# Three column blocks of an out-projection kept in PSUM until the third mixer joins, and x moved on GpSimd's queue

## The chip, the cores and the metric
The kernel runs on one core of one Trainium2 chip. The metric is the time of one execution in microseconds (us), and less is better. The time before is the median of three runs.

## The reference
An encoder of two layers works on 512 tokens of width 1024. Each layer has two halves: a mixer half, with three token mixers side by side, and a feed-forward half, dense in layer 0 and two of eight experts in layer 1. The change concerns the end of the mixer half, from the merged mixers to the residual x.

```python
def rms_norm(x, g):
    xf = x.astype(jnp.float32)
    y = xf * lax.rsqrt(jnp.mean(xf * xf, axis=-1, keepdims=True) + EPS)
    return (y * g.astype(jnp.float32)).astype(x.dtype)
...
    merged = jnp.concatenate([
        rms_norm(o_ssm, out_norm[:e1]),
        rms_norm(o_mla.astype(h.dtype), out_norm[e1:e2]),
        rms_norm(o_fox.astype(h.dtype), out_norm[e2:]),
    ], axis=-1)
    return merged @ w_out
...
    for i in range(DEPTH):
        ada = c_act @ w_ada[i] + b_ada[i]
        sh1, sc1, g1, sh2, sc2, g2 = jnp.split(ada, 6, axis=-1)

        h = modulate(rms_norm(x, norm_mix[i]), sh1, sc1)
        mix = hybrid_mixer(h, cos, sin, w_in[i],
...
        x = x + g1[:, None, :] * mix

        h = modulate(rms_norm(x, norm_ffn[i]), sh2, sc2)
        j = i // 2
        if i % 2 == 0:
            ff = swiglu(h, ffn_w_gate[j], ffn_w_up[j], ffn_w_down[j])
        else:
            ff = moe_ffn(h, moe_w_router[j], moe_b_router[j], moe_w_gate[j], moe_w_up[j], moe_w_down[j])
        x = x + g2[:, None, :] * ff
```

The mixers are S5 (o_ssm, width 256), latent attention (o_mla, 384) and forgetting attention (o_fox, 384). Together they make 1024 columns, which are eight blocks of 128: blocks 0 and 1 are S5, 2 to 4 latent attention, 5 to 7 forgetting attention.

## The kernel before
x is kept with its features on the partitions: eight column blocks of 128 partitions by 512 tokens, 256 KB each. A product in full precision is three matmuls (mm3, L397 and L400 to L402): the weights' high half wh by the activations' high half mg0 and low half mg1, and the weights' low half wl by mg0. The weights come raw from DRAM on SyncE's queue into wr, ScalarE casts them to wh (L383), and VectorE subtracts to get wl (L384); there are two buffers each of wh and wl.

The out-projection is done in two parts, because two mixers are ready before the third.
- In the first part, step "w,d" of a list written by hand (SEQ), for each column block d: a load of x's block from where the layer's input lies (xsrc, L1273), 15 matmuls over the five blocks of the mixers that are ready, a gated add of x (L1280) and a write of the sum into a DRAM tensor xs (L1281). The loads and writes are issued on ScalarE's queue. Three tiles, sA, sB and sC, take turns.
- The third mixer (latent attention) is normalised and merged by g,M (L406 to L417, L953, L961 to L963). The sum over its squares is L953, its first reader is L406 on ScalarE.
- In the second part x's eight blocks are loaded from xs (L1300, ScalarE's queue), and for each d nine matmuls over the third mixer's three blocks go into a bank, which is added, gated, into x (L1309).

Behind it, layer 0 squares x (L493), adds the squares (L495) and sums them over the partitions on TensorE (L498) for the next norm. In layer 1 the router is fed block by block (route: L1594 the router's product, L1596 transposes, L1598 to L1603 what reads them). moe_ahead, called ahead of the second part, loads the router's weights on GpSimd's queue (L1553), makes vec from the adaLN values (L1557, L1559), ws from the weights (L1561), multiplies ws by ones (L1565, ws's bank is read into brt by L1567), and transposes vec into vt, which goes through DRAM (L1573 to L1578).

During the last attention units and the out-projection, layer 0 also streams the adaLN weights: 512 KB a load on SyncE's queue, one VectorE instruction each (L478).

PSUM has eight banks, in four tags with 2, 3, 2 and 1 bank: A, B, C and D. A step names its tag, or bank() takes the next one of a cycle. The Tile scheduler orders the instructions of each engine under what the lists and priorities give it; it is the program text that is changed here, and the order follows.

Of the kernel before, what the change touches and what calls it, by code (L numbers as in the profile page):

```python
# [21 lines left out]
P = 128  # L22
D = 1024
L = 512
DEPTH = 2
KD = D // P
# [27 lines left out]
def _most_blocks():  # L54
# [4 lines left out]
    while todo:  # L59
# [12 lines left out]
NIT = NE  # L72
WST = 200
# [31 lines left out]
SEQ = ("""k,BBAD v,BD f,0,B p,0,4,1 f,1,A p,4,4,0 R l s,0 A s,1 m,0 A a,16,25 s,2 f,2,C A s,3 a,25,26 A o m,1 A m,2 a,26,34 g,F,A g,5,D a,34,40 A w,0,C g,M,A w,1,C w,2,C w,3,C w,4,C w,5,A w,6,C w,7,D""",  # L105
       """k,AACC R f,0,B s,0 s,1 v,A l f,1,C s,2 m,0 A A f,2,B s,3 A m,1 A o m,2 A g,F,C g,5,C A g,M,B w,0,A w,1,C w,2,B w,3,C w,4,C w,5,C w,6,C w,7,C""")
# [180 lines left out]
class Net:  # L287
# [889 lines left out]

    def layer_mix(self, l, xsrc, x, xst):

        nc, tc, a = self.nc, self.tc, self.a  # L1180
        v = nc.vector
        with ExitStack() as st:
# [4 lines left out]
            ps = self.norm_sum(x, (0, 2, 4, 6)) if l == 0 else None  # L1187
# [7 lines left out]
            with ExitStack() as st2:  # L1195
# [3 lines left out]
                units, env = [], {}  # L1199
# [71 lines left out]
                def out(d, side):  # L1271
                    xt = env["far"].tile([P, L], FT, tag="s" + "ABC"[d % 3], name="xs", bufs=1)
                    nc.scalar.dma_start(out=xt, in_=xsrc[:, d])  # L1273
                    hi, lo = self.wload(a["wofs"][l, d], 5 * P)
                    ps = self.bank(side)
                    for kk in range(5):
                        k = (5, 6, 7, 0, 1)[kk]
                        s = slice(kk * P, (kk + 1) * P)
                        self.mm3(ps, (hi[:, s], lo[:, s]), tuple(m_[:, k] for m_ in env["mg"]), kk == 0, kk == 4)
                    v.scalar_tensor_tensor(out=xt, in0=ps, scalar=g1[:, d:d + 1], in1=xt, op0=OP.mult, op1=OP.add)  # L1280
                    nc.scalar.dma_start(out=xs[:, d, :], in_=xt)  # L1281

                do = dict(k=gates, v=values, f=fox, p=mats, R=open_far, a=ada, s=s5, o=s5_out, l=mla_low,
                          m=mla, A=att, g=merge, w=out)
# [14 lines left out]
            for k in range(KD):  # L1299
                nc.scalar.dma_start(out=x[:, k], in_=xs[:, k, :])  # L1300
            for d2 in range(KD // 2):
                hi, lo = self.wload(a["wom"][l, d2], 6 * P)
                for d in (2 * d2, 2 * d2 + 1):
                    ps = self.bank()
                    for kk in range(3):
                        c = (d % 2) * 3 + kk
                        s = slice(c * P, (c + 1) * P)
                        self.mm3(ps, (hi[:, s], lo[:, s]), tuple(m_[:, 2 + kk] for m_ in mg), kk == 0, kk == 2)
# [634 lines left out]
```

## Time and profile before

| | |
|---|---|
| time, median of 3 runs | 1590.76 us (1585.99 to 1594.48) |
| profiled execution | 1596.47 us, span 1594.8 us |
| granted TensorE clock, mean | 0.951 |
| TensorE busy | 1473.1 us, 92% |
| VectorE busy | 1108.4 us, 70% |
| ScalarE busy | 794.6 us, 50% |
| GpSimd busy | 154.3 us, 10% |

The profiled execution has its own time. The span is the time from its first to its last instruction, and all the starts below are counted from the span's start. An engine's waiting time stands ahead of the instruction that ended it, with what it is put down to. The clock is in shares of full speed: 1.00 is 2.4 GHz, 0.50 is 1.2 GHz, and a number between is a mean over the window.

### The profile page before, as it was taken

What the parts mean: (1) busy time and instruction counts of PE and PEld (TensorE: products, weight loads), DVE (VectorE), ACT (ScalarE), POOL (GpSimd) and SP (SyncE); (2) the same over time, 40 slices, a digit from 0 to 9 for tenths busy, and PEclk for the clock granted to TensorE, in tenths of its full rate; (3) what the DMA queues carried; (4) which work ended last, traced back from release to release, by engine and by line L of the source; (5) the groups of instructions that cost most, each with busy time, mean ns of one, the idle gap of its engine ahead of it and who ended that gap; (6) DMA issues with size and microseconds to landing.
All of it is one profiled execution on the core that took longest, in us unless ns stands there. A gap on an engine that the chain in (4) does not pass through costs nothing.

```text
span 1594.8 us, 24065 instructions
## 1 busy us (share of the span) xinstructions
PE 1473.1 (92%) x8331; PEld 1223.5 (77%) x8331; DVE 1108.4 (70%) x2522; ACT 794.6 (50%) x1525; POOL 154.3 (10%) x238
## 2 busy tenths in 40 slices
PE   6889888879999999999999999679999999999996
PEld 5877665658888788887878657568878998998894
DVE  7685678766855577555446565678777878878885
ACT  4245368343332233233435862357556766776672
POOL 0312210011000000003111000110000001002002
PEclk7989999989999999999989999789999999999997
DMA  9423432655566656553421006277777878879885
GB/s 351 145 91 132 151 104 75 224 211 158 173 210 193 223 181 224 181 166 106 130 80 55 21 1 204 86 255 283 250 267 282 307 242 299 321 265 334 281 293 195
DMA packets 94720, 308.87 MB, mean 194 GB/s; under 512 B 12144, under 2 KB 12592, under 8 KB 94592
## 3 DMA queue, kind: packets, MB, share of 16 engines
q1 hardware_dynamic: 74880, 253.42, 47.0%
q0 software_dynamic: 12800, 41.26, 7.6%
q10 hardware_dynamic: 6912, 12.59, 2.3%
q8 instruction: 68, 1.11, 0.3%
q14 instruction: 60, 0.49, 0.1%
HBM read 283.43 MB, written 23.79 MB: 193 GB/s over the span
## 4 chain that ended last, share of the span: by engine, by line
PE 55%; DMA 13%; DVE 13%; issue 11%; ACT 6%; POOL 1%; ACTq 0%; SPq 0%; DVEq 0%; POOLq 0%
PE psB L401 5%; PE psB L402 4%; PE psB L400 4%; DMA adw<-in_wada_dram 4%; PE psC L401 3%; PE psC L400 3%; PE psC L402 3%; PE psA L401 3%; PE psA L400 3%; PE psA L402 3%; DMA wr<-in_mw_dram 2%; DVE wl L384 2%; PE psB L1461 2%; DVE adw L478 2%; PE psA L877 1%
## 5 line engine op out<-in xcount | busy, mean ns | idle before, releaser
L383 ACT CAST wh<-wr 128x1024 fp32r<-128x1024 f32 (+4 forms) x402 | 395.4, 993 | 433.8 <-PE psB L401 82.5
L384 DVE TENSOR_TENSOR wl<-wr,wh 128x1024 fp32r<-128x1024 f32 (+4 forms) x402 | 457.7, 1148 | 153.9 <-ACT wh L383 151.0
L478 DVE SCALAR_TENSOR_TENSOR adw<-adw,cact 128x1024 f32<-128x1024 f32 x80 | 97.8, 1223 | 78.2 <-DMA adw<-in_wada_dram 78.0
L877 PE MATMUL psA<-U 65*128 65x128 f32 (+5 forms) x192 | 74.8, 476 | 16.6 <-ACT pr L881 8.5
L1461 PE MATMUL psB<-hgB,wh 128*128 128x432 f32 (+3 forms) x256 | 80.4, 323 | 0.2
L880 DVE TENSOR_REDUCE ms<-psA 128x1 f32<-128x128 f32 (+2 forms) x96 | 46.2, 486 | 49.4 <-PE psA L878 49.0
L1463 PE MATMUL psB<-hgB,wl 128*128 128x256 f32 x256 | 71.2, 284 | 0.6 <-DVE wl L384 0.6
L400 PE MATMUL psB<-fh,wh 128*128 128x512 f32 (+1 forms) x156 | 61.2, 392 | 4.7 <-ACT fh L518 4.7
L881 ACT ACTIVATE pr<-psA,ms 128x128 f32<-128x128 f32 (+2 forms) x96 | 51.9, 544 | 25.2 <-DVE ms L880 25.0
L1461 PE MATMUL psC<-hgB,wh 128*128 128x432 f32 (+3 forms) x192 | 61.2, 324 | 1.7 <-ACT wh L383 1.6
L401 PE MATMUL psB<-fh,wh 128*128 128x512 f32 (+1 forms) x156 | 61.0, 391 | 0.8 <-POOL fh L521 0.5
L402 PE MATMUL psB<-fh,wl 128*128 128x512 f32 (+1 forms) x156 | 60.5, 388 | 0.0
L1461 PE MATMUL psA<-hgB,wh 128*128 128x432 f32 (+3 forms) x184 | 58.9, 326 | 0.2 <-ACT wh L383 0.2
L1463 PE MATMUL psC<-hgB,wl 128*128 128x256 f32 x192 | 54.0, 284 | 3.1 <-DVE wl L384 2.9
L877 PEld LDWEIGHTS psA<-U 65*128 65x128 f32 (+1 forms) x192 | 32.6, 205 | 26.2 <-ACT pr L881 13.0
L1463 PE MATMUL psA<-hgB,wl 128*128 128x256 f32 x184 | 51.8, 283 | 0.3 <-DVE wl L384 0.3
L894 ACT COPY PT<-psB 128x384 f32<-128x384 f32 (+1 forms) x72 | 37.2, 530 | 26.8 <-PE psB L891 26.4
L1461 PEld LDWEIGHTS psB<-hgB,wh 128*128 128x128 f32 x256 | 48.5, 190 | 2.0 <-ACT wh L383 1.1
L1463 PEld LDWEIGHTS psB<-hgB,wl 128*128 128x128 f32 x256 | 48.4, 189 | 1.3 <-DVE wl L384 0.8
L1541 POOL DMA_DIRECT2D yd<-yt x21 | 11.8, 564 | 376.2 <-ACT yt L1531 265.6
L891 PE MATMUL psB<-cst,pr 128*128 128x128 f32 x240 | 42.6, 285 | 5.9 <-ACT pr L881 4.8
L891 PEld LDWEIGHTS psB<-cst,pr 128*128 128x128 f32 x240 | 28.0, 146 | 24.1 <-issue 11.1
(774 smaller groups left out, 4300.5 us busy)
## 6 DMA issues: line engine op xcount, KB each, us to landing
wr<-in_mw_dram SPq DMA_DIRECT2D x158, 512.0 KB, 4.5
adw<-in_wada_dram SPq DMA_DIRECT2D x80, 512.0 KB, 3.5
wr<-in_md_dram SPq DMA_DIRECT2D x80, 512.0 KB, 4.3
wr<-in_fg_dram SPq DMA_DIRECT2D x22, 512.0 KB, 4.0
wr<-in_fu_dram SPq DMA_DIRECT2D x22, 512.0 KB, 4.0
wr<-in_me_dram SPq DMA_DIRECT2D x16, 512.0 KB, 4.6
wr<-in_w_f_dram SPq DMA_DIRECT2D x12, 512.0 KB, 3.5
wr<-in_fd_dram SPq DMA_DIRECT2D x16, 384.0 KB, 3.1
```

Of the source, the lines that this page charges most:

```text
L383: nc.scalar.copy(hi[:, :n], raw[:, :n])
L384: nc.vector.tensor_tensor(out=lo[:, :n], in0=raw[:, :n], in1=hi[:, :n], op=OP.subtract)
L400: mm(ps, a[0], b[0], start=start, stop=False, skip_group_check=shared)
L401: mm(ps, a[0], b[1], start=False, stop=False, skip_group_check=shared)
L402: mm(ps, a[1], b[0], start=False, stop=stop, skip_group_check=shared)
L478: nc.vector.scalar_tensor_tensor(out=w, in0=w, scalar=1.0, in1=self.cact, op0=OP.mult, op1=OP.mult, accum_out=self.ada[l][:, j:j + 1])
L877: nc.tensor.matmul(ps[:, s], U[0:r, 2 + hh, i * P:n], U[0:r, hh, 0:n], start=True, stop=False)
L880: v.reduce_max(out=m, in_=ps[:, s], axis=AX.X, negate=True)
L881: nc.scalar.activation(pr[:, s], ps[:, s], AF.Exp, bias=m, accum_out=ls[:, hh, i:i + 1])
L891: nc.tensor.transpose(ps[:, c * P:(c + 1) * P], pr[:, o:o + P], self.C("ident"))
L1461: mm(ps[:, :2 * C], hi[:, s], h2, start=(kk == 0), stop=False, skip_group_check=True)
L1463: mm(ps[:, C:C + 2 * P], lo[:, s], h2[:, 0:2 * P], start=False, stop=(kk == KD - 1), skip_group_check=True)
```

## The change
In both layers the first part is done in steps for blocks 0 to 4 alone (NWX is 5). For blocks 5, 6 and 7 its 15 matmuls are issued right behind the x loads, by the new out_first, into banks with the tags B, C and A, without the flag that ends a sum. In the second part the nine matmuls of those blocks go on in the same bank, and their gated add takes x from its source. So for three blocks the load of x into a tile of the first part, the gated add there, and the write to xs are gone. All moves of x at this place (loads and writes of the first part, eight loads of the second) are issued on GpSimd's queue.

```diff
@@ -102,8 +104,8 @@
-SEQ = ("""... A w,0,C g,M,A w,1,C w,2,C w,3,C w,4,C w,5,A w,6,C w,7,D""",
-       """... g,M,B w,0,A w,1,C w,2,B w,3,C w,4,C w,5,C w,6,C w,7,C""")
+SEQ = ("""... A w,0,C g,M,A w,1,C w,2,C w,3,C w,4,C""",
+       """... g,M,B w,0,A w,1,C w,2,B w,3,C w,4,C""")
@@ -1175,6 +1177,14 @@
+    def out_first(self, ps, l, d, mg, stop=False):
+
+        hi, lo = self.wload(self.a["wofs"][l, d], 5 * P)
+        for kk in range(5):
+            k = (5, 6, 7, 0, 1)[kk]
+            s = slice(kk * P, (kk + 1) * P)
+            self.mm3(ps, (hi[:, s], lo[:, s]), tuple(m_[:, k] for m_ in mg), kk == 0, stop and kk == 4)
@@ -1270,15 +1280,11 @@
                 def out(d, side):
                     xt = env["far"].tile([P, L], FT, tag="s" + "ABC"[d % 3], name="xs", bufs=1)
-                    nc.scalar.dma_start(out=xt, in_=xsrc[:, d])
-                    hi, lo = self.wload(a["wofs"][l, d], 5 * P)
+                    nc.gpsimd.dma_start(out=xt, in_=xsrc[:, d])
                     ps = self.bank(side)
...
+                    self.out_first(ps, l, d, env["mg"], True)
                     v.scalar_tensor_tensor(out=xt, in0=ps, scalar=g1[:, d:d + 1], in1=xt, op0=OP.mult, op1=OP.add)
-                    nc.scalar.dma_start(out=xs[:, d, :], in_=xt)
+                    nc.gpsimd.dma_start(out=xs[:, d, :], in_=xt)
@@ -1297,15 +1303,21 @@
             for k in range(KD):
-                nc.scalar.dma_start(out=x[:, k], in_=xs[:, k, :])
+                nc.gpsimd.dma_start(out=x[:, k], in_=xs[:, k, :] if k < NWX else xsrc[:, k])
+
+            whole = {}
+            for d in range(NWX, KD):
+                whole[d] = self.bank("BCA"[d - NWX])
+                self.out_first(whole[d], l, d, mg)
             for d2 in range(KD // 2):
                 hi, lo = self.wload(a["wom"][l, d2], 6 * P)
                 for d in (2 * d2, 2 * d2 + 1):
-                    ps = self.bank()
+                    ps = whole[d] if d in whole else self.bank()
...
-                        self.mm3(ps, (hi[:, s], lo[:, s]), tuple(m_[:, 2 + kk] for m_ in mg), kk == 0, kk == 2)
+                        self.mm3(ps, (hi[:, s], lo[:, s]), tuple(m_[:, 2 + kk] for m_ in mg),
+                                 kk == 0 and d not in whole, kk == 2)
```

The lines move down by two above out_first and by some twelve below it: L384 becomes L386, L1281 becomes L1287, L1309 becomes L1321, L1565 becomes L1577.

What the change does to VectorE's order in layer 0, at the third mixer's merge (oM is that mixer's output, ada with adw the adaLN stream, L407 to L417 its norm); before:

```order
L417 SCALAR_TENSOR_TENSOR nr<-ntmp,nr 128x512
L478 SCALAR_TENSOR_TENSOR adw,ada_111<-adw,cact 128x1024
L961 SCALAR_TENSOR_TENSOR oM<-oM,sm_107,nr 128x512 x3
L1280 SCALAR_TENSOR_TENSOR xs<-psA,ada_111,xs 128x512
L384 TENSOR_TENSOR wl<-wr,wh 128x640
L963 TENSOR_TENSOR mg_2836<-oM,mg_2835 128x512 x2
L1280 SCALAR_TENSOR_TENSOR xs<-psC,ada_111,xs 128x512
L963 TENSOR_TENSOR mg_2836<-oM,mg_2835 128x512
L478 SCALAR_TENSOR_TENSOR adw,ada_111<-adw,cact 128x1024
L384 TENSOR_TENSOR wl<-wr,wh 128x768
L1280 SCALAR_TENSOR_TENSOR xs<-psD,ada_111,xs 128x512
L384 TENSOR_TENSOR wl<-wr,wh 128x768
```

and with the change:

```order
L419 SCALAR_TENSOR_TENSOR nr<-ntmp,nr 128x512
L480 SCALAR_TENSOR_TENSOR adw,ada_111<-adw,cact 128x1024
L963 SCALAR_TENSOR_TENSOR oM<-oM,sm_107,nr 128x512 x3
L386 TENSOR_TENSOR wl<-wr,wh 128x640
L965 TENSOR_TENSOR mg_2836<-oM,mg_2835 128x512 x2
L480 SCALAR_TENSOR_TENSOR adw,ada_111<-adw,cact 128x1024
L965 TENSOR_TENSOR mg_2836<-oM,mg_2835 128x512
L386 TENSOR_TENSOR wl<-wr,wh 128x768 x2
L480 SCALAR_TENSOR_TENSOR adw,ada_111<-adw,cact 128x1024
L1321 SCALAR_TENSOR_TENSOR x<-psA,ada_111,x 128x512
```

The three gated adds of blocks 5 to 7 (L1280) are gone; the subtraction for block 7's weights (128x640) stands directly behind L963, which was L961.

TensorE's order in layer 1 around the router's ws (psB_9037 is block 1 of the second part); before:

```order
L400 MATMUL psB_9037<-mg0_8520,wh_9008 128x512
L401 MATMUL psB_9037<-mg1_8521,wh_9008 128x512
L402 MATMUL psB_9037<-mg0_8520,wl_9009 128x512
L1565 MATMUL psC_8973<-ws8_8967,ones_69 128x8 x8
L1571 MATMUL psC_8984<-cst_95,vec_8968 16x128
L1596 MATMUL psA_9048<-cst_95,x_8960 128x128 x4
L1594 MATMUL psD_8996<-wr8_8965,x_8960 128x8 x8
L1596 MATMUL psC_9023<-cst_95,x_8960 128x128 x4
```

and with the change (psA_8957 holds block 7's and psC_8935 block 6's first part):

```order
L402 MATMUL psA_8957<-mg0_8505,wh_8960 128x512
L403 MATMUL psA_8957<-mg1_8506,wh_8960 128x512
L404 MATMUL psA_8957<-mg0_8505,wl_8961 128x512
L1577 MATMUL psC_8880<-ws8_8874,ones_69 128x8 x8
L1583 MATMUL psC_8891<-cst_95,vec_8875 16x128
L402 MATMUL psC_8935<-mg0_8505,wh_8938 128x512
L403 MATMUL psC_8935<-mg1_8506,wh_8938 128x512
L404 MATMUL psC_8935<-mg0_8505,wl_8939 128x512
```

The ws matmuls stood behind all of the first part and two blocks of the second, and now stand behind block 7's first part and ahead of block 6's.

GpSimd's queue in layer 1; before:

```order
L1021 COPY xn<-nld 128x2
L1022 MEMSET xn 128x2
L1553 DMA wr_8965<-in_wr_dram 128x64
L1575 DMA vd<-vt 16x128
L1578 DMA vrow_8990<-vd 128x1024
L1578 DMA vrow_8991<-vd 128x1024
```

and with the change:

```order
L1024 MEMSET xn 128x2
L1283 DMA xs<-xd 128x512 x3
L1287 DMA xs_6441<-xs 128x512 x2
L1283 DMA xs<-xd 128x512 x2
L1287 DMA xs_6441<-xs 128x512 x3
L1565 DMA wr_8872<-in_wr_dram 128x64
L1306 DMA x<-xs_6441 128x512 x5
L1306 DMA x<-xd 128x512 x3
L1587 DMA vd<-vt 16x128
L1590 DMA vrow_8897<-vd 128x1024
L1590 DMA vrow_8898<-vd 128x1024
```

The router's weights (wr) are now issued behind all the writes into xs and ahead of the loads of x; vd and vrow follow these.

## Rows read from the trace of the kernel before

**Rows 1.** The page, part 1: busy time, share of the span and instructions of each engine.
```profile
PE 1473.1 (92%) x8331; PEld 1223.5 (77%) x8331; DVE 1108.4 (70%) x2522; ACT 794.6 (50%) x1525; POOL 154.3 (10%) x238
```

**Rows 2.** Timeline of ScalarE, layer 0: start, us, engine line operation, idle before <-releaser.
```profile
301.18 0.72 ACT L383 CAST wh<-wr 128x640 fp32r<-128x640 f32 x1 [7.02 <-DMA xs<-xs]
...
325.52 5.62 ACTq L1300 DMA_DIRECT2D x<-xs  x8
331.26 0.84 ACT L383 CAST wh<-wr 128x768 fp32r<-128x768 f32 x1 [5.22 <-DMA x<-xs]
```

**Rows 3.** Timeline of TensorE, layer 0, same columns.
```profile
297.31 1.02 PE L953 MATMUL psA<-sq,ones 128*128 128x512 f32 x2
...
314.43 0.80 PE L402 MATMUL psD<-mg,wl 128*128 128x512 f32 x1 [3.12 <-DVE wl L384]
...
319.72 0.63 PE L402 MATMUL psD<-mg,wl 128*128 128x512 f32 x1
320.14 0.45 PE L400 MATMUL psA<-mg,wh 128*128 128x512 f32 x1
...
336.51 0.39 PE L402 MATMUL psB<-mg,wl 128*128 128x512 f32 x1
339.45 1.12 PE L498 MATMUL psA<-sq,ones 128*128 128x512 f32 x2 [2.56 <-DVE sq L495]
342.03 5.49 PE L498 MATMUL psA<-sq,ones 128*128 128x512 f32 x6 [1.45 <-DVE sq L495]
```

**Rows 4.** Windows, layer 0: busy PE, PEld, DVE, ACT, POOL; PEclk, DMA share, GB/s.
```profile
302.00:310.00 8.00, 7.09 (x27) 4.90 (x28) 6.13 (x10) 2.49 (x4) 0.00 (x0) 1.00 0.91 282
315.00:320.00 5.00, 5.00 (x13) 3.91 (x12) 3.85 (x6) 0.00 (x0) 0.00 (x0) 0.50 0.65 212
342.00:347.50 5.50, 5.47 (x6) 1.85 (x6) 0.00 (x0) 0.63 (x1) 0.00 (x0) 0.50 0.21 83
```

**Rows 5.** Timeline of VectorE, layer 0.
```profile
309.76 1.23 DVE L478 SCALAR_TENSOR_TENSOR adw<-adw,cact 128x1024 f32<-128x1024 f32 x1 [1.62 <-DMA adw<-in_wada_dram]
...
312.90 0.74 DVE L1280 SCALAR_TENSOR_TENSOR xs<-psA,ada,xs 128x512 f32<-128x512 f32 x1
...
316.16 0.68 DVE L963 TENSOR_TENSOR mg<-oM,mg 128x512 fp32r<-128x512 f32 x1
...
330.82 0.75 DVE L1309 SCALAR_TENSOR_TENSOR x<-psA,ada,x 128x512 f32<-128x512 f32 x1 [2.23 <-DMA x<-xs]
...
341.29 0.68 DVE L495 TENSOR_TENSOR sq<-sq 128x512 f32<-128x512 f32 x1
```

**Rows 6.** Windows of layer 1, columns as in rows 4.
```profile
740.00:957.00 217.00, 208.33 (x1413) 165.24 (x1412) 121.65 (x356) 121.33 (x303) 31.62 (x62) 0.95 0.20 65
994.00:998.00 4.00, 4.00 (x22) 4.00 (x20) 0.06 (x1) 0.26 (x1) 1.62 (x3) 0.50 0.05 17
```

**Rows 7.** Timeline of TensorE, layer 1.
```profile
990.27 3.58 PE L1565 MATMUL psC<-ws,ones 128*128 128x8 f32 x16 [3.60 <-DVE ws L1561]
...
1020.58 0.31 PE L1596 MATMUL psC<-cst,x 128*128 128x128 f32 x1
```

**Rows 8.** Timeline of VectorE, layer 1.
```profile
974.20 0.73 DVE L1280 SCALAR_TENSOR_TENSOR xs<-psC,ada,xs 128x512 f32<-128x512 f32 x1
...
985.74 0.17 DVE L1557 SCALAR_TENSOR_TENSOR vec<-ada,sm 128x8 f32<-128x8 f32 x1 [1.30 <-DMA xs<-xs]
...
989.99 0.23 DVE L1561 TENSOR_TENSOR ws<-wr,ada 128x64 f32<-128x64 f32 x1 [0.44 <-DMA wr<-in_wr_dram]
```

**Rows 9.** Timeline of GpSimd, layer 1.
```profile
986.35 0.54 POOL L1553 DMA_DIRECT2D wr<-in_wr_dram  x1 [108.78 <-DVE vec L1559]
```

**Rows 10.** Part 6, DMA issues: count, KB each, median us from issue to landing.
```profile
xs<-xs ACTq DMA_DIRECT2D x16, 256.0 KB, 2.7
x<-xs ACTq DMA_DIRECT2D x16, 256.0 KB, 6.4
```

**Rows 11.** Lines of GpSimd: busy time, mean ns of one, idle before and releasers.
```profile
L1389 POOL DMA_DIRECT2D xd<-x x8 | 4.3, 539 | 97.0 <-DVE ada L481 55.1 <-DVE x L1384 41.9
```

More of the change, by code (lines that the diff above doesn't have):

```diff
@@ L72 @@
 NIT = NE
+NWX = 5
 WST = 200
@@ L104 @@
 FIRST = (("w_vu", NVU, FSD), ("w_f0", 256, "B"))
-SEQ = ("""k,BBAD v,BD f,0,B p,0,4,1 f,1,A p,4,4,0 R l s,0 A s,1 m,0 A a,16,25 s,2 f,2,C A s,3 a,25,26 A o m,1 A m,2 a,26,34 g,F,A g,5,D a,34,40 A w,0,C g,M,A w,1,C w,2,C w,3,C w,4,C w,5,A w,6,C w,7,D""",
-       """k,AACC R f,0,B s,0 s,1 v,A l f,1,C s,2 m,0 A A f,2,B s,3 A m,1 A o m,2 A g,F,C g,5,C A g,M,B w,0,A w,1,C w,2,B w,3,C w,4,C w,5,C w,6,C w,7,C""")
+SEQ = ("""k,BBAD v,BD f,0,B p,0,4,1 f,1,A p,4,4,0 R l s,0 A s,1 m,0 A a,16,25 s,2 f,2,C A s,3 a,25,26 A o m,1 A m,2 a,26,34 g,F,A g,5,D a,34,40 A w,0,C g,M,A w,1,C w,2,C w,3,C w,4,C""",
+       """k,AACC R f,0,B s,0 s,1 v,A l f,1,C s,2 m,0 A A f,2,B s,3 A m,1 A o m,2 A g,F,C g,5,C A g,M,B w,0,A w,1,C w,2,B w,3,C w,4,C""")
 ADN = (2, 2)
@@ L1272, in out @@
                     xt = env["far"].tile([P, L], FT, tag="s" + "ABC"[d % 3], name="xs", bufs=1)
-                    nc.scalar.dma_start(out=xt, in_=xsrc[:, d])
-                    hi, lo = self.wload(a["wofs"][l, d], 5 * P)
+                    nc.gpsimd.dma_start(out=xt, in_=xsrc[:, d])
                     ps = self.bank(side)
[L1276 to L1279, printed above, removed]
+                    self.out_first(ps, l, d, env["mg"], True)
                     v.scalar_tensor_tensor(out=xt, in0=ps, scalar=g1[:, d:d + 1], in1=xt, op0=OP.mult, op1=OP.add)
-                    nc.scalar.dma_start(out=xs[:, d, :], in_=xt)
+                    nc.gpsimd.dma_start(out=xs[:, d, :], in_=xt)
                 do = dict(k=gates, v=values, f=fox, p=mats, R=open_far, a=ada, s=s5, o=s5_out, l=mla_low,
```

## The prediction

> **What bounds the kernel now.** The page's first part comes first: TensorE is busy 92% of the span, VectorE 70% and GpSimd 10% [rows 1]. So an edit that leaves the matmuls as they are can pay only where TensorE waits, or where it runs at the lower of its two clock levels (1.2 and 2.4 GHz). Then I read the ends of the two out-projections, where the change sits, engine by engine and in windows; the reader should look for three things.
>
> First, the queue. In layer 0 ScalarE stands at issues of x moves: a cast at 301.18 waits 7.02 us, put down to xs's DMA, and with it the norm's L406 behind it, though TensorE had written the sum that L406 reads by 298.33; later the eight issues at 325.52 hold ScalarE until a cast at 331.26, which is put down to x's DMA [rows 2, 3]. Second, VectorE. TensorE waits 3.12 us for w7's wl (314.43) and then runs at clock 0.50, after 1.00 between 302 and 310 with waits under 1 us [rows 3, 4]. VectorE was held by an adaLN stream instruction that waited 1.62 us for its load, by three merges and by a gated add (312.90) [rows 5]. Behind the out-projection VectorE is 5.07 us late: TensorE ends at 336.90, but the first add into x waits for x until 330.82, so the last sum of squares ends at 341.97, and the norm's matmuls, again at 0.50, end at 347.52 [rows 3 to 5].
>
> Third, layer 1. The router's weights (wr) are loaded when vec is written, vec waits for the writes into xs, and TensorE waits 3.60 us for ws until 990.27; the window behind it stands at 0.50, and so do its neighbours from 990.2 to 1002.7. TensorE ends at 1020.89 [rows 6 to 8].
>
> **The change part by part.** Matmuls and weight loads stay the same in number. Per layer three loads, three writes and three adds of 0.74 us go; that is VectorE's time, and counts only where it stands ahead of a wait. Five loads, five writes and eight x loads go from ScalarE's queue to GpSimd's, which was idle 108.78 us before its next issue in layer 1 [rows 9]. Each plain issue costs GpSimd 0.54 us [rows 11]; 36 cost it 19 us, hidden by that idle time. The whole blocks hold three banks, so blocks 0 to 4 have fewer to turn over in; each needs one for nine matmuls and an add of 0.74 us, and with five banks left (four in layer 1, where the router holds one) I cost that at nothing (uncovered, it would be 0.74 a block, 3.7 us a layer).
>
> *Layer 0, ahead of the third mixer's part.* One gated add, 0.74 us, leaves VectorE in front of w7's wl, and the adaLN load could be earlier by up to its wait of 1.62 [rows 5]. So wl is ready 0.7 to 2.3 us earlier and TensorE waits 0.8 to 2.4 instead of 3.12. Whether the clock falls then is open: at a spacing of 0.42 (319.72 to 320.14) instead of 0.23 (72 matmuls from 320.14 to 336.90) twelve matmuls lose 2.3 us. The third part starts at 320.14 before, and after between 315.5 (all of it) and 319.4 (the least); I take 317.5, about half of each.
>
> *Layer 0, to the norm.* The third part took 16.76 us for its 72 matmuls, eight blocks of 2.1, without a wait that matters: TensorE ends at 332.3 to 336.2, I take 334.3. The x loads no longer wait for writes of blocks 5 to 7. What releases them is the third merge (done at 316.84 before [rows 5], some 0.8 earlier without the add), so they are issued around 316 and land 2.7 us later, like the moves from xs to xs, or 6.4, like the eight at once before [rows 10]: 318.7 to 322.4, about when the first block is ready (319.6). VectorE then follows TensorE and is late by the last add, square and sum alone, some 0.7 us each, 2.1 instead of 5.07. The last sum ends at 334.4 to 338.3, I take 336.4 (341.97 before). The norm's matmuls behind it may keep their 5.49 us or be rid of the half clock. Gain 3.7 to 8.5 us; I take **6**.
>
> *Layer 1.* ScalarE is freed here too, but TensorE has no wait in blocks 3 to 7, so I take nothing. After w4 (986.67, where its wait began, less two blocks of 2.1 and three of 15 matmuls, 3.45 each: 972.2) come the first parts of blocks 5 and 7. Block 7's weights need the buffer of the high half that block 5 frees, and VectorE's wl: I count 1.0 us of waiting, so it ends at 980.1. Meanwhile w4's add, at 974.20 before [rows 8], is the last one written to xs; its write lands 2.7 us after its issue [rows 10], at about 977.2; vec and the wr issue follow, and ws comes 3.6 us on (986.35 to 989.99 before [rows 8, 9]): at 981.2 instead of 990.2. TensorE waits 1.1 us instead of 3.60. The ws matmuls, 3.58 us at half clock [rows 7], take 1.8 at full: 983.0. Block 6 starts in their bank after VectorE has read it: 0.5. From the ws matmuls to its end TensorE took 27.04 us before (993.85 to 1020.89) for six third parts and eight router parts; 4.4 of it went to half clock until 1002.7, so 22.6. After: 983.0 + 0.5 + 3.45 for block 6 + 4.2 for two more third parts + 22.6 = 1013.8, and 0.8 for a cast and x0 that come late: 1014.6, plus h. The kernel before loses 6.2 us by half clock (12.5 us of it); h lies between nothing and that, since waits under 1 us leave 1.00 in layer 0 [rows 4] and waits from 2.56 us on stand ahead of 0.50 [rows 3, 4]. My waits are 0.5 to 1.1 us, nearer to the first; I take h = 1.3. I leave 1 us for router parts that now follow each other more closely and end VectorE's work later. Gain -1 to 5.3; I take **4**.
>
> **Sum:** 6 + 4 = 10 us. The profiled execution of 1596.47 (span 1594.8) becomes 1586.5; it lies 5.7 above the median of 1590.76, from which the same 10 us give **1581**. The bounds, 3.7 - 1 and 8.5 + 5.3, are 2.7 and 13.8 us: 1577 to 1588. Half a per cent, 8 us, is about what can be told from no change here: the runs of before spread over 8.5.
>
> **A rule that speaks against it.** GpSimd's eight issues of L1389 took 0.54 us on average beside a VectorE that is busy 70% of the span [rows 11, 1]. The Trainium skill ("SBUF — State Buffer", sections "SBUF: two separate sides" and "A bandwidth-pool intuition that's wrong") says that the descriptors of a DMA issued from GpSimd are written by GpSimd, which some VectorE operations lock out of a shared port; it gives 620 ns alone and 3100 ns overlapped, and advises ScalarE's or SyncE's queue. By its second figure the eight x loads of layer 0 would be issued over 25 us instead of 4.3 (estimate), and the gain would be gone; the rows agree with the first figure, and none here shows the second.
>
> **The rivals.**
> *One layer only.* The other stall is handed on: in layer 1 the clock falls anyway, h = 6 (for it: wr's 3.6 us stand in the chain whatever frees it, and three waits follow each other; against: the load starts 9 us earlier), or in layer 0 the adaLN loads set w7's wl as now. Gain 3 to 7, 1584 to 1588; I say 1586.
> *No gain to be seen.* Three bank calls fewer per layer deal out all later banks otherwise, and the instructions of layer 1's attention and of the experts move. From 740 to 957 and from 1042 to the end that is 48% of the span. In the first of these TensorE is idle 8.7 us [rows 6]; half as much again, and one half-clock stretch of 4 us as in [rows 6], eats 8 of the 10: 1588 to 1594, I say 1590.
> *Slower: GpSimd's issues are held.* If each waits for two VectorE instructions like the adaLN stream's 1.23 us [rows 5], it takes 0.54 + 2.46 = 3.0 us. Layer 0's eight loads, in order from 316, then land by 316 + 24 + 2.7 = 342.7, and the norm's last sum is done by 344.8, 2.8 later than before. In layer 1 the write of w4 and the wr load stand one behind the other on this queue: ws comes 4.9 us later than I have it, TensorE ends at 1014.6 + 4.9 + 6 = 1025.5, 4.6 later. Together +7: 1598. It decides from 2.7 us an issue, at which layer 0's last x (340.3) gives the last sum of before. Against it: the 0.54 of [rows 11]. Behind these moves on the queue stand only s5w in layer 0 and vd in layer 1, both needed later.
> *More than I think.* Both drops of the clock gone, and the norm's matmuls at full clock: 14 to 18 us, 1573 to 1577.
>
> **How the numbers follow.** Both layers near my values (1577 to 1585) 0.50; one layer only 0.22; no gain to be seen 0.13; slower 0.08; more 0.07. The bound for faster, 1582.8, cuts the first case near its upper quarter: 0.40 of it, all of the last and 0.05 of the second are 0.52. Slower by 8 us, 1598.7, is half of the slow case and a little of the third: 0.06. The rest is 0.42. The range goes from 1573 to 1593 and leaves out the slow case, the worst of the third and a little below the last. The likeliest case's own range is 1577 to 1585.
>
> **What would show it.** Right: in layer 0 no issue on ScalarE's queue ahead of L406, a wait of TensorE for w7's wl under 2.5 us, x landed within 3 us of the first block, the last sum within 3 us of TensorE's end; in layer 1 the wr issue near 977, a wait at the ws matmuls under 2 us and the clock at 1.00 behind it; issues of x moves of 0.5 to 0.6 us. Wrong: issues of 2 us and more; a wait of 3 us at ws or at block 6; clock 0.50 in either stretch; more waits of TensorE in layer 1's attention or in the experts than before.

## The result, and the profile after

The changed kernel took 1574.61 us, the median of four executions (1569.99 to 1585.06); the kernel before, in four beside it, 1592.62. The ratio is 0.9893, with a 95% interval of 0.9858 to 0.9927: 17 us less, and between 12 and 23. Six more executions later (E5 below) gave 0.9892. The profiled execution of the changed kernel took 1585.06 us with a span of 1583.4, the longest of those four.

The page's first part after the change, to stand against [rows 1]:

```profile
PE 1464.8 (93%) x8331; PEld 1217.8 (77%) x8331; DVE 1105.2 (70%) x2516; ACT 795.0 (50%) x1525; POOL 179.3 (11%) x274
```

The same 8331 matmuls kept TensorE busy for 8.3 us less. A matmul takes longer at the lower clock (the norm's last six took 5.49 us at 0.50 [rows 3, 4] and take 2.84 at 1.00, below), so time that the clock costs stands in the busy time, not in the waits.

For a table by stage I cut each execution at the same five instructions of ScalarE: the first square of the third mixer's output in layer 0 (L952, at 286.64 before), the first L406 of the feed-forward norm (347.55), the first L406 of layer 1 (730.25), the first square of the third mixer's output there (955.48) and the last square of the router's parts (1020.92). The windows before (busy time and count of TensorE, its weight loads, VectorE, ScalarE and GpSimd; then granted clock, DMA share, GB/s):

```profile
0.00:286.64 286.64, 239.50 (x1545) 191.33 (x1546) 211.96 (x695) 146.26 (x364) 47.18 (x85) 0.92 0.44 150
286.64:347.55 60.91, 52.63 (x191) 35.58 (x189) 37.30 (x58) 19.20 (x33) 4.21 (x9) 0.89 0.77 262
347.55:730.25 382.70, 376.08 (x1696) 310.31 (x1696) 241.72 (x520) 118.49 (x178) 19.61 (x25) 0.99 0.57 181
730.25:955.48 225.23, 212.73 (x1416) 169.86 (x1418) 130.16 (x375) 126.11 (x312) 32.51 (x62) 0.94 0.20 64
955.48:1020.92 65.44, 61.55 (x305) 51.29 (x301) 35.99 (x59) 20.31 (x34) 2.15 (x4) 0.90 0.43 141
1020.92:1594.80 573.88, 530.59 (x3182) 465.11 (x3182) 451.27 (x818) 364.21 (x607) 48.65 (x53) 0.96 0.78 273
```

And the changed kernel, cut at the same instructions:

```profile
0.00:290.77 290.77, 245.73 (x1545) 195.60 (x1546) 212.86 (x695) 145.93 (x365) 48.71 (x90) 0.89 0.43 148
290.77:344.26 53.49, 48.04 (x191) 34.11 (x189) 35.05 (x55) 19.62 (x33) 11.78 (x22) 0.97 0.79 271
344.26:730.28 386.02, 378.58 (x1696) 312.74 (x1696) 242.22 (x520) 118.41 (x177) 20.41 (x25) 0.98 0.57 180
730.28:945.88 215.60, 203.52 (x1417) 164.10 (x1418) 129.63 (x375) 126.85 (x313) 36.34 (x65) 0.98 0.21 68
945.88:1004.96 59.08, 57.26 (x305) 46.43 (x302) 34.98 (x57) 20.07 (x34) 10.18 (x19) 0.98 0.40 129
1004.96:1583.40 578.44, 531.63 (x3182) 464.84 (x3181) 450.41 (x816) 364.07 (x607) 51.87 (x53) 0.96 0.77 271
```

The two stages that the change was made in are 7.4 and 6.4 us shorter. So is one in which no line was changed: layer 1's norm, mixers and attention, 225.23 to 215.60. Three came out longer: the first by 4.1, layer 0's feed-forward (the third row) by 3.3 and the last by 4.6. The reader should look at the clock beside each length: 0.89 to 0.97, 0.94 to 0.98, 0.90 to 0.98 in the three stages that gained, and 0.92 to 0.89 in the first, in which TensorE's instructions stand in the same order in both.

Now the rows that answer to those of before. ScalarE in layer 0, to stand against [rows 2]:

```profile
301.41 0.72 ACT L385 CAST wh<-wr 128x640 fp32r<-128x640 f32 x1 [3.10 <-PE psC L403]
302.50 0.69 ACT L408 ACTIVATE ntmp<-psA,eps 128x512 f32<-128x512 f32 x1 [0.37 <-PE psA L955]
```

Both wait for TensorE; no x move stands in the queue. TensorE there, against [rows 3]:

```profile
311.53 0.50 PE L404 MATMUL psC<-mg,wl 128*128 128x512 f32 x1 [1.77 <-DVE wl L386]
...
334.40 0.50 PE L404 MATMUL psC<-mg,wl 128*128 128x512 f32 x1 [1.23 <-DVE wl L386]
...
341.38 2.84 PE L500 MATMUL psB<-sq,ones 128*128 128x512 f32 x6 [0.78 <-DVE sq L497]
```

Before, the wait of 3.12 us was for the low half of block 7's weights. Block 7's first part, from 316.21, now has no wait over 0.5 us; the 1.77 us stand in block 6's, and 1.23 came for a low half of the third part, so that together they are 3.00. The norm's last six matmuls took 2.84 instead of 5.49, at the higher clock. VectorE, against [rows 5]:

```profile
324.86 0.75 DVE L1321 SCALAR_TENSOR_TENSOR x<-psA,ada,x 128x512 f32<-128x512 f32 x1 [1.64 <-DMA x<-xs]
...
340.64 0.68 DVE L497 TENSOR_TENSOR sq<-sq 128x512 f32<-128x512 f32 x1
```

TensorE's last block ended at 337.87, and the last sum of squares 3.45 us behind it instead of 5.07. In layer 1 the issue of the router's weights, against [rows 9]:

```profile
968.10 0.54 POOL L1565 DMA_DIRECT2D wr<-in_wr_dram  x1 [2.63 <-DMA xs<-xs]
```

And the ws matmuls, against [rows 7]:

```profile
966.78 0.50 PE L402 MATMUL psA<-mg,wh 128*128 128x512 f32 x1 [0.59 <-ACT wh L385]
...
970.97 1.95 PE L1577 MATMUL psC<-ws,ones 128*128 128x8 f32 x16
```

The wait of 3.60 us is gone, and the sixteen matmuls took 1.95 instead of 3.58 us. The GpSimd lines of x's moves (busy time, mean ns of one, idle before and releasers):

```profile
L1287 POOL DMA_DIRECT2D xs<-xs x10 | 5.4, 544 | 91.0 <-DVE xs L1286 90.8
...
L1306 POOL DMA_DIRECT2D x<-xs x10 | 5.3, 539 | 8.9 <-PE psA L404 8.9
...
L1283 POOL DMA_DIRECT2D xs<-in_xT_dram x5 | 2.7, 539 | 32.1 <-PE psD L857 21.2 <-DVE o L861 7.8 <-DMA xs<-xs 2.9
```

No issue was held: all 36 took 0.54 us on the mean.

### The profile page after: what moved, and what is told of

It reads as the page before. It is cut to its first block, busy times and chain, and to the rows that moved or that the text cites. A ratio compares the mean times of both kernels' runs of the same rounds, so it can differ in the third digit from the quotient of the medians.

```text
span 1583.4 us, 24058 instructions
## 1 busy us (share of the span) xinstructions
PE 1464.8 (93%) x8331; PEld 1217.8 (77%) x8331; DVE 1105.2 (70%) x2516; ACT 795.0 (50%) x1525; POOL 179.3 (11%) x274
## 3 DMA queue, kind: packets, MB, share of 16 engines
q1 hardware_dynamic: 74880, 253.42, 47.1%
## 4 chain that ended last, share of the span: by engine, by line
PE 36%; DMA 5%; DVE 5%; ACT 2%; issue 2%; POOL 0%; DVEq 0%; SPq 0%; ACTq 0%; POOLq 0%
DMA wr<-in_mw_dram 2%; PE psB L1473 2%; PE psB L403 2%; PE psB L404 2%; PE psB L402 2%; PE psC L1473 2%; DVE wl L386 2%; PE psB L1475 2%; PE psA L1473 1%; PE psC L404 1%; PE psC L403 1%; PE psC L402 1%; PE psA L403 1%; PE psA L404 1%; PE psA L402 1%
## 5 line engine op out<-in xcount | busy, mean ns | idle before, releaser
L386 DVE TENSOR_TENSOR wl<-wr,wh 128x1024 fp32r<-128x1024 f32 (+4 forms) x402 | 457.8, 1149 | 155.3 <-ACT wh L385 146.7
L1473 PE MATMUL psB<-hgB,wh 128*128 128x304 f32 (+3 forms) x264 | 83.0, 325 | 0.1
L883 ACT ACTIVATE pr<-psA,ms 128x128 f32<-128x128 f32 (+2 forms) x96 | 51.5, 540 | 16.8 <-DVE ms L882 16.3
L1473 PE MATMUL psC<-hgB,wh 128*128 128x432 f32 (+3 forms) x176 | 56.6, 327 | 2.6 <-ACT wh L385 2.6
L1473 PE MATMUL psA<-hgB,wh 128*128 128x432 f32 (+3 forms) x168 | 53.1, 323 | 2.0 <-ACT wh L385 2.0
L1553 POOL DMA_DIRECT2D yd<-yt x21 | 11.8, 565 | 376.3 <-ACT yt L1543 264.0
L1473 PEld LDWEIGHTS psB<-hgB,wh 128*128 128x128 f32 x264 | 50.3, 191 | 1.9 <-ACT wh L385 1.0
L1475 PEld LDWEIGHTS psB<-hgB,wl 128*128 128x128 f32 x264 | 50.2, 190 | 2.0 <-DVE wl L386 1.5
L1475 PE MATMUL psA<-hgB,wl 128*128 128x256 f32 x168 | 47.4, 285 | 3.1 <-DVE wl L386 3.0
L1475 PE MATMUL psC<-hgB,wl 128*128 128x256 f32 x176 | 49.7, 286 | 0.0
L893 PEld LDWEIGHTS psB<-cst,pr 128*128 128x128 f32 x240 | 29.4, 152 | 21.7 <-issue 12.5
```

The source lines that it names most:

```text
L386: nc.vector.tensor_tensor(out=lo[:, :n], in0=raw[:, :n], in1=hi[:, :n], op=OP.subtract)
L883: nc.scalar.activation(pr[:, s], ps[:, s], AF.Exp, bias=m, accum_out=ls[:, hh, i:i + 1])
L893: nc.tensor.transpose(ps[:, c * P:(c + 1) * P], pr[:, o:o + P], self.C("ident"))
L1473: mm(ps[:, :2 * C], hi[:, s], h2, start=(kk == 0), stop=False, skip_group_check=True)
L1475: mm(ps[:, C:C + 2 * P], lo[:, s], h2[:, 0:2 * P], start=False, stop=(kk == KD - 1), skip_group_check=True)
```

## The experiments

Each was timed beside the kernel before. To read them I took from each profile the three stages named above (layer 0's end, layer 1's attention, layer 1's end) and the experts, as windows between the same instructions. The table gives each one's length and in brackets TensorE's waits in it, which is the window less TensorE's busy time; what is left is busy time of the same matmuls in every row, so where that differs it is the clock. All in us. The kernels with TensorE's old order in layer 1's attention stand above, those with the new one below.

| kernel | layer 0's end | layer 1's attention | layer 1's end | experts |
|---|---|---|---|---|
| before | 60.9 (8.3) | 225.2 (12.5) | 65.4 (3.9) | 573.9 (43.3) |
| E8 banks shifted | 57.9 (9.0) | 219.4 (12.6) | 65.3 (3.9) | 577.0 (46.2) |
| E7 layer 1, banks as before | 62.1 (11.3) | 221.8 (12.7) | 59.4 (3.2) | 574.6 (45.8) |
| E1 layer 1 alone | 64.3 (11.4) | 219.4 (12.7) | 59.2 (3.1) | 578.7 (49.7) |
| E3 queue alone | 57.0 (6.5) | 217.2 (11.9) | 63.9 (4.2) | 572.8 (43.6) |
| E4 hold alone | 54.9 (7.7) | 214.6 (11.9) | 62.4 (3.6) | 574.7 (44.7) |
| E2 layer 0 alone | 52.4 (5.7) | 217.2 (13.0) | 67.0 (7.8) | 577.1 (46.8) |
| changed | 53.5 (5.5) | 215.6 (12.1) | 59.1 (1.8) | 578.4 (46.8) |
| E5 changed, again | 52.5 (5.3) | 215.7 (11.8) | 60.1 (1.9) | 575.8 (45.4) |
| E6 changed, banks as before | 52.7 (5.8) | 218.8 (12.3) | 59.2 (3.1) | 578.0 (46.0) |

**E1: the change in layer 1 alone.** Layer 0 keeps its eight steps and ScalarE's queue:

```diff
-NWX = 5
+NWX = (8, 5)
...
-                    nc.gpsimd.dma_start(out=xt, in_=xsrc[:, d])
+                    (nc.gpsimd if NWX[l] < KD else nc.scalar).dma_start(out=xt, in_=xsrc[:, d])
```

> The change in layer 1 alone; layer 0 as before. The order of TensorE in layer 1's attention is then word for word that of the kernel before. Theory (the two ends of the out-projections gain 7.4 and about 6.5 us, and a new order of instructions in layer 1's attention, which the change in layer 0 brings about, gains another 10): only the second end gains here, 5 to 7 us, ratio 0.996, and the stretch from layer 1's first norm to its merges (730 to 955 us) takes as long as before. Rival (the attention's stretch differs from execution to execution, whatever the order): that stretch comes out up to 10 us shorter in this profile too. Second rival (layer 1's end is given back in the experts): ratio 1.000.

Measured: ratio 1.0015 (0.9989 to 1.0041), median 1593.95 us. Layer 1's end fell to 59.2 us, as the theory has it, and the experts rose to 578.7, as the second rival has it. The attention's stretch, with the old order of TensorE, came out at 219.4 instead of 225.2: so part of the 9.6 us between the first two profiles is chance.

**E2: the change in layer 0 alone**, with NWX of (5, 8).

> The change in layer 0 alone; layer 1's out-projection as before. TensorE's order in layer 1's attention is that of the changed kernel. Theory: 7 us at layer 0's end and about 10 in layer 1's attention, less some 2 in between: 13 to 16 us, ratio 0.991. Rival (the attention's gain is chance): 5 to 7 us, ratio 0.996.

Measured: ratio 0.9969 (0.9944 to 0.9994), median 1584.67. Layer 0's end (52.4) and the attention (217.2) gained what the theory says, but the total is nearer to the rival's. Part of what is missing stands in the experts, 577.1 (3.2 us more than before), as in E1, and part in layer 1's end, 67.0 (1.6 more), where one wait is now twice as long as the 3.60 us of before:

```profile
973.28 3.55 PE L1577 MATMUL psC<-ws,ones 128*128 128x8 f32 x16 [7.32 <-DMA x<-xs]
```

Why it grew was not tried. Much of the rest is the measure: the profile of before that these lengths are held against is of an execution of 1596.47 us, 4.9 above the median of 1591.62 that E2 was timed beside.

**E3: the queue alone.** The eight blocks stay as before:

```diff
-                    nc.scalar.dma_start(out=xt, in_=xsrc[:, d])
+                    nc.gpsimd.dma_start(out=xt, in_=xsrc[:, d])
...
-                    nc.scalar.dma_start(out=xs[:, d, :], in_=xt)
+                    nc.gpsimd.dma_start(out=xs[:, d, :], in_=xt)
...
-                nc.scalar.dma_start(out=x[:, k], in_=xs[:, k, :])
+                nc.gpsimd.dma_start(out=x[:, k], in_=xs[:, k, :])
```

> Only the queue is changed: all moves of x at this place on GpSimd's queue, all eight blocks as before. TensorE's order in layer 1's attention is that of the changed kernel. Theory: the attention's 10 us, and at layer 0's end 1 to 3 us, since ScalarE is no longer held at the issues, but x still waits for the writes of blocks 5 to 7: 10 to 13 us, ratio 0.993. Rival (the blocks held in PSUM do it all): within 3 us of before. Second rival (GpSimd's issues are held while VectorE works): issues of x moves of 2 us and more, slower by 5.

Measured: ratio 0.9954 (0.9933 to 0.9974), median 1584.44. The second rival is out: the 48 issues of x moves took 0.54 us on the mean, and the kernel is not slower. Of the two ends it gains part, 57.0 and 63.9 us, 0.9 and 1.4 us under the shortest of the kernels whose end there is that of before (57.9 and 65.3); the attention is at 217.2.

**E4: the three blocks held, all moves on ScalarE's queue** (the same three lines the other way round in the changed kernel).

> Only the three blocks are held in PSUM; all moves of x stay on ScalarE's queue. TensorE's order in layer 1's attention is that of the changed kernel. Theory: the attention's 10 us, and of the two ends some 4 us each, since x of blocks 5 to 7 needs no write any more, but ScalarE still stands at issues: 16 to 18 us, ratio 0.990, at most 3 us behind the changed kernel. Rival (the queue does it): within 3 us of before.

Measured: ratio 0.9926 (0.9899 to 0.9953), median 1580.25. Both ends lie between before and the changed kernel (54.9, 62.4). By these profiles, one of each, the hold is the larger part, the queue adds to it, and neither does the whole; the intervals of E3 and E4 overlap.

**E5: the changed kernel again.**

> The changed kernel once more, beside the next three on the same chip, with more executions than its first four. Theory: its parts as the profiles of the first experiments give them are 7 to 10 us at layer 0's end, some 6 in layer 1's attention and 6.5 at layer 1's end, less what the experts lose: 13 to 18 us, ratio 0.990. Rival (the first four executions were lucky, and the parts add up as layer 0 alone and layer 1 alone were timed, 5 us together): ratio 0.997.

Measured: ratio 0.9892 (0.9858 to 0.9927), median 1574.13. The rival is out.

**E6: the changed kernel with its later banks dealt out as before:**

```diff
                 for d in (2 * d2, 2 * d2 + 1):
+                    if d in whole:
+                        self.side += 1
                     ps = whole[d] if d in whole else self.bank()
```

> The changed kernel, but each block held in PSUM moves the bank cycle on by one, so that all later banks are dealt out as before; TensorE's order in the experts is again that of before, but for a few places. Theory (the three bank calls that each changed layer leaves out shift the experts' banks, and this costs 3 to 5 us there): the experts' stretch falls from 578.4 to about 574 us, the time to some 1571, ratio 0.987. Rival (the experts' stretch differs by chance): like the changed kernel within 2 us, and its stretch anywhere from 573 to 579.

Measured: ratio 0.9888 (0.9846 to 0.9930), median 1574.40; the experts' stretch 578.0. The theory fails here: with the six calls put back the experts gain nothing against the changed kernel's 575.8 and 578.4.

**E7: layer 1 alone, with banks as before** (E1 with the two lines of E6).

> The change in layer 1 alone, with the bank cycle moved on as in the run before: order of layer 1's attention and of the experts both as before. Theory: what is left is layer 1's end, 6 to 7 us, ratio 0.996, the experts' stretch at 574 us instead of the 578.7 of layer 1 alone, without waits of 4 us for yf near its end. Rival (the end's gain is given back in the experts whatever the banks): ratio 1.000 as for layer 1 alone.

Measured: ratio 0.9988 (0.9966 to 1.0011), median 1589.11, between theory and rival. The experts' stretch is 574.6 and the wait for yf is gone, as the theory says; of the 6 us of layer 1's end some 2 show in the time, with an interval from a gain of 5.4 us to a loss of 1.8.

**E8: the bank shift alone**, in the kernel before:

```diff
                     if l == DEPTH - 1:
                         self.route(x[:, d], d)
+            if l == 1:
+                self.side -= 3
```

> The kernel before with nothing changed but the bank cycle set back by three behind layer 1's out-projection, as leaving out three bank calls in one layer does. Only the order in the experts differs, and it is that of layer 0 alone. Theory: the experts' stretch rises from 573.9 to 577 or 579 us, with a wait of 4 to 5 us for yf near its end; slower by 3 to 5 us, ratio 1.0025. Rival (chance): ratio 1.000 and no such wait.

Measured: ratio 1.0036 (1.0003 to 1.0068), median 1594.34. Nothing was left out and no instruction of the out-projection moved, and the time rose. The wait foretold is there:

```profile
1555.70 0.47 PE L1528 MATMUL psB<-cst,yf 128*128 128x128 f32 x1 [4.54 <-DVE yf L1522]
```

The same order of the experts, and a wait of 4.35 and 5.32 us at the same line, stand in E2 and E1. So a shift by three banks, which one changed layer makes, costs the experts some 4 us (577.0 to 578.7 in these three, 572.8 to 574.6 in before, E3 and E7); two changed layers shift by six, have another order, and have no such wait. That is part of why the layers alone do not add up to both: E2's gain of 4.9 us, E7's of 1.9 and the 5.7 that E8 lost make 12.5 of the 17, each with an interval of several us, and E2's wait of 7.32 us stands in neither before nor the changed kernel.

**E9 to E11: more blocks held.** A fourth in layer 0 (E9), a fourth and fifth in layer 0 (E10), a fourth in both (E11). The lines of E9, to which the steps left out of layer 0's list belong:

```diff
-NWX = 5
+NWX = (4, 5)
+WHB = ("BCAD", "BCA")
...
-                whole[d] = self.bank("BCA"[d - NWX])
+                whole[d] = self.bank(WHB[l][d - NWX[l]])
```

> The changed kernel with a fourth block, 4, held in PSUM in layer 0 (tag D): one load, one write and one gated add less there. Theory (layer 0's end is set by x's transfers and by VectorE's order, and each block held takes 0.74 us and two transfers of 256 KB away): layer 0's end 1 to 2 us shorter than the changed kernel's 52.5 to 53.5, the experts with their banks set back by seven and so unknown within 3 us: ratio to before 0.986 to 0.991. Rival (what is left there is TensorE's own work and the wait for weights): layer 0's end as in the changed kernel, ratio 0.989.

> The same with blocks 3 to 7 held in layer 0 (tags B, C, A, D, B). Three banks are left to blocks 0 to 2 of the second part; the experts' order is that of before. Theory: layer 0's end 2 to 4 us shorter than in the changed kernel, ratio 0.986. Rival (the banks run out: TensorE waits for gated adds of blocks 0 to 2, which wait for x): layer 0's end as long as in the changed kernel or longer by up to 3 us.

> Four blocks held in both layers (tags B, C, A, D in layer 0 and B, C, A, B in layer 1); the experts' order is that of before, but for a few places. Theory: layer 0's end as with four blocks there; in layer 1 the last write into xs is one block earlier, so the router's weights come 3 us earlier, but TensorE no longer waits for them, so its end stays at 59 to 60 us; ratio 0.986. Rival (two banks of B are held, and the router's parts wait for banks): layer 1's end 1 to 4 us longer.

Measured: ratios 0.9910 (0.9876 to 0.9943), 0.9912 (0.9883 to 0.9942) and 0.9911 (0.9878 to 0.9944). Layer 0's end took 51.3, 51.0 and 52.3 us against 52.4 to 53.5 with three blocks: at most 1 to 2 us, and none of it in the time. Layer 1's end took 62.2 us in E11 against 59.1 to 60.1, as its rival has it. The experts took 580 to 581 us in all three, more than in any other kernel. Why is not settled; their banks are set back by seven or eight, and by eight the order of TensorE there is all but that of before, which took 573.9. So that order alone does not set the stretch's length.

**E12: the adaLN stream earlier.**

```diff
-... a,25,26 A o m,1 A m,2 a,26,34 g,F,A ...
+... a,25,30 A o m,1 A m,2 a,30,34 g,F,A ...
```

> The changed kernel with four of the adaLN stream's instructions moved from the stretch behind the last attention units to that ahead of them, so that the stream's last instruction stands ahead of the third mixer's merge on VectorE. Theory (what is left of waiting at layer 0's end comes from adaLN loads, one at a time, ahead of the weights' low halves on VectorE): no waits of TensorE for wl there, layer 0's end 2 to 5 us shorter than 52.5 to 53.5, of which the attention ahead may take back 1 to 3; the stretch of layer 1's attention is ordered a little otherwise, unknown within 4 us; ratio 0.985 to 0.990. Rival (x's transfers set that end): no shorter than 52 us, ratio 0.989 or more.

Measured: ratio 0.9900 (0.9869 to 0.9931). Layer 0's end fell to 47.7 us, and no wait of TensorE over 1 us is left in its third part. So the stream, not x's loads, set what was left there; its loads and its instructions on VectorE, which E12 moves together, it cannot tell apart. But all ahead of that stage took 293.2 us, where the thirteen other profiles lie between 282.5 and 290.8, and the time is that of the changed kernel. The trace says where that time went. Four of the stream's instructions now stand on VectorE between 218 and 236 us, and there TensorE waits as in no other profile:

```profile
227.67 2.07 PE L879 MATMUL psA<-U 65*128 65x512 f32 x2 [3.84 <-ACT pr L883]
```

TensorE's matmuls 1201 to 1500, which hold this place, took 63.4 us with 10.4 of waits; in the thirteen other profiles they took 54.3 to 56.1 with 6.6 to 6.9. The excess, 7.3 us at the least, is more than the 4.8 to 5.8 that layer 0's end gained. The wait is put down to ScalarE's pr; how the moved instructions hold that was not followed.

**What the attention's gain is.** All kernels in which layer 0's end was changed have the new order of TensorE in layer 1's attention, and none of the others. The stretch took 219.4 to 225.2 us in the four profiles of the old order and 214.6 to 218.8 in the six below them: means of 221.4 and 216.5. TensorE's waits in it sum to 12.6 us on the mean with the old order and 12.2 with the new. Of the 4.9 us 4.5 are busy time of the same matmuls, so the clock. In the old order, in all four profiles, TensorE has two waits that the new one lacks, of 1.74 to 1.75 and 2.15 to 2.16 us; in the kernel before:

```profile
836.25 0.65 PE L996 MATMUL psC<-cst,xn 128*65 128x128 f32 x4 [1.75 <-DVE xn L1019]
...
927.17 0.66 PE L891 MATMUL psB<-cst,pr 128*128 128x128 f32 x4 [2.15 <-ACT pr L881]
```

and the windows behind them:

```profile
840.00:846.00 6.00, 6.00 (x20) 4.46 (x21) 1.45 (x6) 2.61 (x7) 0.99 (x3) 0.51 0.12 36
927.00:931.00 4.00, 3.83 (x24) 2.65 (x26) 3.61 (x15) 0.81 (x4) 0.00 (x0) 0.60 0.00 0
```

Behind both the clock is lower in all four profiles. The new order has waits of its own, of 1.41, 1.51 to 1.52 and 1.14 to 1.15 us, in all six.

In E5 the first of them stands ahead of a lower clock:

```profile
815.98 1.11 PE L893 MATMUL psB<-cst,pr 128*128 128x128 f32 x4 [1.41 <-ACT pr L883]
```

```profile
816.00:820.00 4.00, 4.00 (x28) 3.10 (x30) 3.11 (x14) 1.17 (x2) 0.96 (x3) 0.63 0.00 0
...
866.00:872.00 6.00, 6.00 (x31) 4.27 (x30) 3.97 (x9) 5.53 (x16) 0.00 (x0) 1.00 0.01 3
```

Behind the second, 1.51 us until 865.05, the clock stayed at 1.00, and in the changed kernel's first profile it stayed there behind the 1.41 too. That the two waits of the old order are what brought the clock down is read from where they stand; a kernel with the old order but without them was not run.

## Why the prediction was right, and where its sum was not

The forecast was 1581 us, a gain of 10 made up of 6 and 4, in a range of 1573 to 1593. Measured were 1574.6, a gain of 17: the sign and the range held, and the sum was short by 7. The time lies below the likeliest case's own 1577 to 1585 and in the span of the last rival, *more than I think* (1573 to 1577), which I gave 0.07. The ends of the two out-projections, from which that rival takes its 14 to 18 us, gained 14.4 (below). Its condition, no drop of the clock left, held in part: in layer 0's end 3.4 us at half clock are left in the first profile after and none in E2, E5 and E6; layer 1's end keeps some in the first profile after and in E5.

**Layer 0's end: right in mechanism, too small.** The steps are in the rows: no x move ahead of L408; x's issue at 319.91, which is 315.8 by the clock of the kernel before (forecast 316). Two are not as I had them. The issue's wait is put down to TensorE's matmuls of block 7's first part (8.9 us, the L1306 line above) and not to the third merge. And the wait for w7's wl, which I left at 0.8 to 2.4 us, is gone in the first profile after (0.8 in E5), but one of 1.77 came a block earlier and one of 1.23 in the third part, so earlier low halves gave little: over the profiles the waits for wl there of 0.6 us and more sum to 3.1 to 4.0 us with the old end and 2.1 to 3.3 with the new. Counted from the stage's first instruction, TensorE's last block ended 3.2 us earlier (47.1 instead of 50.3; forecast 2.6; 1.2 of it waits and 1.9 the clock), the last sum of squares 4.8 (forecast 5.6), the norm's matmuls 7.4. The last step is the one I left open ("may keep their 5.49 us or be rid of the half clock") and gave 0.4: it is 2.6. Nor did the bound of 8.5 hold it: 341.97 less 334.4 is 7.6, and half of 5.49 makes it 10.3. Over the profiles, four with the old end (mean 61.3) and four with the new (52.8), the gain is 8.5 us where I had 6. Of these TensorE's waits are 4.4 (10.0 to 5.6) and the clock 4.1.

**Layer 1's end: right in mechanism, its allowances too large.** The wr issue was foreseen near 977 and came at 968.10, which is 977.7 by the clock of the kernel before, since all stands 9.6 us earlier. ws followed 2.6 us on instead of 3.6, so TensorE waited not 1.1 us at the ws matmuls but nothing, and the clock stayed up behind it, where [rows 6] had 0.50:

```profile
972.00:976.00 4.00, 3.87 (x22) 3.20 (x22) 0.68 (x2) 0.25 (x1) 1.40 (x3) 1.00 0.98 297
976.00:980.00 4.00, 3.15 (x16) 2.31 (x14) 1.71 (x2) 0.84 (x1) 0.00 (x0) 1.00 0.56 217
980.00:984.00 4.00, 4.00 (x26) 3.48 (x26) 1.43 (x2) 1.91 (x3) 1.08 (x2) 1.00 0.62 209
```

It does not always stay up. In E5 the same ws matmuls, behind a wait of 0.22 us, are followed by 3.4 us at half clock:

```profile
960.00:964.00 4.00, 3.87 (x20) 3.17 (x20) 0.91 (x2) 0.25 (x1) 1.65 (x4) 0.79 1.00 308
964.00:968.00 4.00, 4.00 (x15) 3.23 (x14) 0.49 (x1) 0.84 (x1) 0.00 (x0) 0.78 0.65 246
```

TensorE was busy in this stage for 56.1 to 56.2 us in the three profiles in which the clock was 1.00 throughout (E1, E6, E7), for 57.3 in the first profile after, where it fell in the last 3 us alone, and for 58.2 in E5. So h, which I took as 1.3 us, was between nothing and 2.0, and the 1 us that I left for the router parts was not needed. The mean gain is 6.5 us (65.9 in three profiles to 59.4 in five). TensorE's waits are 2.6 of it and the clock 3.9. Without E2 and its wait of 7.32 us it is 5.9, of which 1.3 are waits and 4.7 the clock.

**Layer 1's attention: the rival named the place and got the sign wrong.** "No gain to be seen" said that moved instructions there could eat 8 of the 10 us by half as many waits again and one half-clock stretch. (By its rows that is 4.35 us of waits and 2 of clock, so 6 rather than 8: a stretch of 4 us at 0.50 holds 2 us of work at 1.00.) The attention gained 4.9 us, with nearly as much waiting in sum; two long waits, with a lower clock behind each, are gone. I priced a reordering at nothing or a loss, and the trace of before had a price for the gain too: a clock of 0.94 over 225 us, some 13 us of it. This is the term that the sum lacked, and that the new order came out on this side of it is luck: nothing in the forecast chose it.

**The experts: part of that rival held, and its size is open.** The two profiles of the changed kernel have 575.8 and 578.4 us there, before and E3 573.9 and 572.8, which is 3.8 us on the mean, and TensorE waits more than before (45.4 and 46.8 us against 43.3), which I had named as a sign of being wrong. With the profiles that have the same order of TensorE in the experts but for a few places, E7 beside before and E3, and E4 (574.7) and E12 (576.0) beside the changed kernel, it is 2.5 us, 573.7 to 576.2. But E6, E10 and E11 took 578.0 to 580.6 with an order that is all but that of before. E8 shows that the order can cost time; what sets it in the changed kernel is not shown. The change in layer 1 alone, of which 5 to 7 us were expected in E1, gave nothing that could be measured, and the shift of the banks is part of that: without the shift (E7) it measured 1.9 us, between a gain of 5.4 and a loss of 1.8.

**One layer only: out.** Both layers' ends gained in every profile of the changed kernel. Its reason for layer 0 has something in it: E12 shows that the adaLN stream sets what is left there.

Layer 0's feed-forward, 3.3 us longer in the first pair of profiles, has means of 384.4 and 384.1 us in the four profiles with the old end ahead of it and the four with the new, so nothing is in it. Together 8.5 + 4.9 + 5.9 - 2.5 is 16.8 us, beside the 17 measured. Each part is a difference of means of few profiles that scatter by 1 to 6 us, so a sum that fits this well is partly luck. The planned terms gained 14.4 where I had 10, and the two unplanned ones, 4.9 and -2.5, add 2.4.

**GpSimd's issues: the rival "slower" is out.** It decided from 2.7 us an issue; measured were 0.54 on the mean of all 36, beside VectorE at work. The Trainium skill ("SBUF — State Buffer", section "A bandwidth-pool intuition that's wrong") gives 620 ns for a DMA issued from GpSimd alone and 3100 ns for one overlapped with a VectorE tensor_copy. These are figures for a whole DMA; the issues of this trace, 0.54 us, show no such hold, and no run here shows the second.

## What to carry to other kernels

Where TensorE is the bound, price a wait by the clock behind it too: in this kernel three stages gained 19 us together (8.5, 4.9 and 5.9), and 13 of them were the same matmuls at the higher clock. Split each stage's length into TensorE's waits and its busy time, before an edit and after. A scheduler's order and a cycle of banks carry an edit into stages that it does not touch, with either sign, so an edit to one of two layers can measure as nothing while both together gain. And look where moved work lands: E12 freed one stage and paid for it in another.

## What the runs showed of the hardware

The first stage, nearly all of it ahead of the change and with TensorE's order the same but for six places at most, took from 282.5 to 290.8 us in the thirteen profiles other than E12's. TensorE was busy in it for 234.6 to 245.7 us and waited 45.0 to 50.2, with the same matmuls. So more of the scatter there is the clock's than the waits'. The thirty executions of the kernel before in the first experiments spread over 22 us.

A wait is no sure sign of the clock behind it. In E5 1.41 us stood ahead of 0.63 and 1.51 us ahead of 1.00; the same wait of 1.41 us stood ahead of 1.00 in the changed kernel's first profile. Behind the ws matmuls the clock was 1.00 after waits of 1.34 us (E1) and 1.40 (E7), and fell to 0.50 for 3.4 us after 0.22 (E5).
